# Token-layout block sums and DMA transposes between the output projection and the up projection

## The chip, the cores and the metric

The kernel runs on one core of a Trainium2 chip. TensorE multiplies, VectorE and ScalarE compute element by element, GpSimd does a few small steps and SyncE (SP) issues most DMAs. Each engine runs its own instructions in order and waits on semaphores for the others. The metric is the device time of one execution in microseconds (us), as the median of several timed runs.

## The reference

One layer of a decoder trunk on x of 1024 tokens by 1024 channels, in float32. What matters here is the seam between the two halves of the layer:

```
merged = sigmoid(g_att) * y_att + sigmoid(g_conv) * y_conv
x = x + rms_norm(merged @ w_out, norm_mix_post)        # output projection

h = rms_norm(x, norm_ffn_pre)
u = causal_dwconv(h @ w_up, conv_ffn_w)                # up projection, 1024 -> 5632
a, g = split(u)
x = x + rms_norm((gelu(g) * a) @ w_down, norm_ffn_post)
```

## The kernel before

**Numbers.** Operands of a product are kept as two float16 parts, a high and a low half: the high half is the value times a power of two (ScalarE writes it), the low half what is left (VectorE writes it). A product takes three passes (high·high, high·low, low·high), so 12 matmuls of 512 columns for a 512x512 block and 128 output channels.

**The up projection** uses seven block products in place of eight. The normalized h is wanted with channels on the partitions: hA holds, in four quadrants (channel half by token half), the plain blocks B11, B21, B22 and the sum T4; hB holds the sums T1, T2, T3. T1 is late minus early tokens of the first channel half, T2 is the second channel half of the late tokens minus T1, T4 the second channel half of the early tokens minus T2, T3 the difference of the late tokens' channel halves. Tokens come in eight tiles of 128: tiles 0 to 3 are the early half, 4 to 7 the late one; tile 4 pairs with tile 0, and so on. `Pair.prod(i)` is one block product; prod(1) and prod(2) read the early quadrants of hA, prod(5), (6) and (7) read T1, T2, T3, prod(3) and prod(4) the late quadrants of hA.

**The stage around the change.** For each tile, `out_proj` runs 48 matmuls into two PSUM banks (py), reading m16_0 to m16_7 (the merged activations) and wo_0 to wo_7 (the weights), in the order of k for each half of the columns. ScalarE squares (L861), VectorE evicts with the gain into hn (L862), r_post comes from GpSimd, x2 is the new residual (L866), stored by SP, and hn becomes the normalized h (L869). `load_xr` fetches the next tile's x on SP.

`blocks(tt, h)` turns that tile: eight TensorE transposes of 128x128 into two PSUM banks (pt), then for an early tile halves written straight into hA (L885, L886), for a late tile the sums T1 to T4 in channel layout, from PSUM and from hA (L893 to L903), with their halves. The list of tiles in the loop sets where the blocks stand: `{2: (0,), 3: (1,), 4: (2,), 5: (3, 4), 6: (5,), 7: (6,)}`, and tile 7's come after the first products of pairs u0 and u1. A scheduler orders the instructions of each engine by its own timeline; the program's order gives the dependences.

**Memory.** `slot()` takes a 4 KB-per-partition tile from one pool, the slab:

```
self.slab = top.enter_context(tc.tile_pool(name="slab", bufs=16))
...
wo_pools = (self.slab, "s", self.slab, "s")
```

At this stage the slab holds the eight tiles of wo, m16_4 to m16_7, the hn tiles, the work tiles of the blocks (tb, hb) and s12, a sum over the weights of the next pair (L969 to L971). A tile gets a slot when an earlier tenant has had its last reader. PSUM has eight banks (pool pz), shared by py, pt and the products (pu).

Of the kernel before, what the change touches and what calls it, by code (L numbers as in the profile page):

```python
# [16 lines left out]
F16 = mybir.dt.float16  # L17
BF16 = mybir.dt.bfloat16
F32 = mybir.dt.float32
I32 = mybir.dt.int32  # L20
AF = mybir.ActivationFunctionType
ALU = mybir.AluOpType
AX = mybir.AxisListType

P = 128
T = 1024
D = 1024
KD = D // P
NH = 512
# [4 lines left out]
KH = KD // 2  # L34
# [3 lines left out]
class Layer:  # L38
# [225 lines left out]
    def mixer(self, mid):  # L264
        tc, nc, a = self.tc, self.nc, self.a
        hT = self.hp.tile([P, 2, KD, T], F16, tag="hT", name="hT")
        with ExitStack() as ph1:
# [33 lines left out]
            with tc.tile_pool(name="ptp", bufs=2, space=bass.MemoryType.PSUM) as ptp:  # L301
                gb = self.slot([P, D], F32, "g_pre")
                xt, rt, pt = {}, {}, {}
# [426 lines left out]
        with ExitStack() as ph2:  # L730

            hB = self.h7p.tile([P, 2, 3, KH, NH], F16, tag="hB", name="hB")
            t4s = []

            def halves(dst, src):
                nc.scalar.activation(dst[:, 0], src, AF.Copy)
                nc.vector.tensor_tensor(dst[:, 1], src, dst[:, 0], ALU.subtract)

            def blocks(q):
                lo, hi = ds(0, NH), ds(NH, NH)  # L740
                kA, kB = ds(2 * q, 2), ds(KH + 2 * q, 2)

                def diff(name, p, m, hT_m=True):

                    t = self.slot([P, 2, NH], F32, f"{name}_{q}")
                    nc.vector.tensor_tensor(t, hT[:, 0, p[0], p[1]], hT[:, 0, m[0], m[1]] if hT_m else m,
                                            ALU.subtract)
                    nc.vector.tensor_tensor(t, t, hT[:, 1, p[0], p[1]], ALU.add)
                    if hT_m:
                        nc.vector.tensor_tensor(t, t, hT[:, 1, m[0], m[1]], ALU.subtract)  # L750
                    return t
                t1 = diff("T1", (kA, hi), (kA, lo))
                halves(hB[:, :, 0, ds(2 * q, 2), :], t1)
                t2 = diff("T2", (kB, hi), t1, False)
                halves(hB[:, :, 1, ds(2 * q, 2), :], t2)
                t4s.append(diff("T4", (kB, lo), t2, False))
                t3 = diff("T3", (kB, hi), (kA, hi))
                halves(hB[:, :, 2, ds(2 * q, 2), :], t3)
# [19 lines left out]

            branches(0, 1, bi=0)
            blocks(0)  # L780
            branches(2, 3, bi=0)
            self.pair_fetch("g1")
            self.inv_h = inv_h
            blocks(1)
            for which in ("gc", "ga"):
                nc.scalar.activation(sig[which, 0], sig[which, 0], AF.Sigmoid)
# [12 lines left out]
            for d in range(1, 8):  # L799
                p = gp[d]  # L800
# [48 lines left out]
        def out_proj(tt):  # L849
# [19 lines left out]
            nc.vector.scalar_tensor_tensor(h, y, r2, gf, ALU.mult, ALU.mult)  # L869
            return h  # L870

        def blocks(tt, h):


            pt = [self.bank(f"pt{tt}_{e}") for e in range(2)]
            for k in range(KD):
                nc.tensor.transpose(pt[k // KH][:, ds((k % KH) * P, P)], h[:, ds(k * P, P)], self.ident)
            sl = ds((tt % 4) * P, P)
            p3 = [p.rearrange("p (k t) -> p k t", k=KH) for p in pt]
            s2 = ds(NH + (tt % 4) * P, P)  # L880
            b11, b21, b22, t4 = hA[:, :, :KH, sl], hA[:, :, KH:, sl], hA[:, :, KH:, s2], hA[:, :, :KH, s2]
            t1, t2, t3 = [hB[:, :, e, :, sl] for e in range(3)]
            if tt < 4:
                for p, b in zip(p3, (b11, b21)):
                    nc.scalar.activation(b[:, 0], p, AF.Copy, scale=s_h2)  # L885
                    nc.vector.scalar_tensor_tensor(b[:, 1], p, s_h2, b[:, 0], ALU.mult, ALU.subtract)  # L886
                return
            tb = [self.slot([P, 2, KH, P], F32, f"tb{tt}_{e}") for e in range(2)]

            def halves(dst, src):  # L890
                nc.scalar.activation(dst[:, 0], src, AF.Copy)
                nc.vector.tensor_tensor(dst[:, 1], src, dst[:, 0], ALU.subtract)
            nc.vector.scalar_tensor_tensor(tb[0][:, 0], p3[0], s_h2, b11[:, 0], ALU.mult, ALU.subtract)  # L893
            nc.vector.tensor_tensor(tb[0][:, 0], tb[0][:, 0], b11[:, 1], ALU.subtract)
            halves(t1, tb[0][:, 0])
            nc.vector.scalar_tensor_tensor(tb[0][:, 1], p3[1], s_h2, tb[0][:, 0], ALU.mult, ALU.subtract)
            halves(t2, tb[0][:, 1])
            hb = self.slot([P, 2, KH, P], F32, f"hb{tt}")
            for e in range(2):
                nc.scalar.activation(hb[:, e], p3[e], AF.Copy, scale=s_h2)  # L900
            nc.vector.tensor_tensor(tb[1][:, 0], hb[:, 1], hb[:, 0], ALU.subtract)
            nc.vector.tensor_tensor(tb[1][:, 1], b21[:, 0], tb[0][:, 1], ALU.subtract)
            nc.vector.tensor_tensor(tb[1][:, 1], tb[1][:, 1], b21[:, 1], ALU.add)  # L903
            halves(b22, hb[:, 1])
            halves(t3, tb[1][:, 0])
            halves(t4, tb[1][:, 1])

        xr = {}

# [4 lines left out]
        hs = {}  # L914
        load_xr(0)
        for tt in range(8):
            if tt + 1 < 8:
                load_xr(tt + 1)
            hs[tt] = out_proj(tt)
            if tt == 0:  # L920
                self.pair_split("u0")
                self.pair_fetch("u1")
            if tt == 3:
                self.pair_sums("u1")
                self.pair_split("u1")
            if tt == 4:
                self.pair_fetch("u2")
            for t in {2: (0,), 3: (1,), 4: (2,), 5: (3, 4), 6: (5,), 7: (6,)}.get(tt, ()):
                blocks(t, hs[t])
# [356 lines left out]
```

## Time and profile before

| what | value |
|---|---|
| timed runs | 1368.22, 1368.27, 1367.43 us; median 1368.22 |
| profiled execution, its own time from first to last instruction (span) | 1365.7 us |
| TensorE busy | 1336.1 us, 98% |
| VectorE busy | 1028.6 us, 75% |
| ScalarE busy | 860.7 us, 63% |
| TensorE's mean granted clock | 0.998 |
| transposes between the projections (L877) | 64 of 272 ns each, started 664.2 to 735.0 |

The times in a profile run from the span's start. A row of a timeline names the start, how long it took, the engine, the line, the operation and what it writes from what. "Busy" of TensorE counts pipelined matmuls that overlap, so the step from one matmul to the next is shorter than its duration. Waits are put down to the engine whose signal came last.

### The profile page before, as it was taken

The page shows a single profiled execution, that of the slowest core. Times are in us where ns is not written, and L with a number is a line of the kernel's source. Part 1 is how long each engine was busy: PE and PEld are TensorE (multiplying, and loading weights), DVE is VectorE, ACT ScalarE, POOL GpSimd, SP SyncE. Part 2 cuts the span into 40 slices and gives each one's busy share as a digit, 9 for nine tenths or more (in the row PEclk, how much of TensorE's full clock was granted, in tenths as well). Part 3 has the DMA queues.
Part 4 walks back from the last instruction along what each step waited for, and adds up shares of the span by engine and source line. Part 5 has one row for each costly group of instructions (what it writes and reads, how often), then busy time and mean ns, then how long its engine had stood idle before and what let it go on. Part 6 is the DMA issues. An engine that isn't in the chain of part 4 may idle for free. (4 is left out here: it accounts for less than half of the span.)

```text
span 1365.7 us, 16990 instructions
## 1 busy us (share of the span) xinstructions
PE 1336.1 (98%) x6651; PEld 607.7 (44%) x6651; DVE 1028.6 (75%) x1610; ACT 860.7 (63%) x1204; POOL 34.2 (3%) x52
## 2 busy tenths in 40 slices
PE   6999999999999999999999999999999999999997
PEld 3444444444444444444454444444444444444443
DVE  6667777777775965878788985984894896699855
ACT  6668778787775775666466577652761673476524
POOL 2000000000000000000010000000000000000002
PEclk9999999999999999999999999999999999999999
DMA  7102111101111121351331123122220321313216
GB/s 264 62 1 62 32 31 32 38 25 39 40 31 47 32 62 31 93 185 36 119 124 62 62 62 123 39 87 85 70 78 16 123 62 62 109 45 124 63 46 109
DMA packets 26576, 96.06 MB, mean 70 GB/s; under 512 B 3072, under 2 KB 3200, under 8 KB 26496
## 3 DMA queue, kind: packets, MB, share of 16 engines
q1 hardware_dynamic: 25056, 89.74, 20.3%
q0 software_dynamic: 1440, 5.24, 2.1%
q8 instruction: 52, 0.85, 0.2%
q14 instruction: 28, 0.23, 0.1%
HBM read 86.58 MB, written 8.39 MB: 70 GB/s over the span
## 5 line engine op out<-in xcount | busy, mean ns | idle before, releaser
L1156 PEld LDWEIGHTS <-wh_u 128*128 128x128 f16 x1848 | 178.8, 98 | 217.3 <-issue 3.5
L1048 PE MATMUL pd<-wdh,f 128*128 128x512 f16 (+1 forms) x1068 | 230.3, 377 | 2.8 <-ACT wdh L86 1.2
L1048 PEld LDWEIGHTS <-f 128*128 128x128 f16 x1068 | 104.4, 98 | 127.2 <-issue 4.3
L86 ACT ACTIVATE wh_u<-ws_u,sc 128x1024 f16<-128x1024 f32 (+1 forms) x66 | 64.7, 998 | 102.9 <-DVE sc L78 79.3
L1055 DVE SCALAR_TENSOR_TENSOR yacc<-pd,sd,yacc 128x512 f32<-128x512 f32 (+1 forms) x81 | 58.5, 740 | 72.7 <-PE pd L1048 65.2
L1156 PEld LDWEIGHTS <-wh_g 128*128 128x128 f16 x588 | 56.9, 98 | 68.7 <-issue 0.4
L859 PE MATMUL py<-wh_wo,m 128*128 128x512 f16 x384 | 83.9, 379 | 0.0
L87 DVE SCALAR_TENSOR_TENSOR wh_u<-ws_u,sc,wh_u 128x1024 f16<-128x1024 f32 (+1 forms) x66 | 72.1, 1099 | 9.5 <-ACT wh_u L86 9.4
L643 DVE SCALAR_TENSOR_TENSOR w<-zc,w 128x1024 f16<-128x1024 f32 (+3 forms) x48 | 45.7, 955 | 34.5 <-ACT w L642 34.4
L622 ACT ACTIVATE sp<-zc 128x1024 f32<-128x1024 f32 (+3 forms) x48 | 40.2, 838 | 46.7 <-DVE zc L615 29.1
L600 PE MATMUL A<-sh,tri 128*128 128x512 f16 (+3 forms) x352 | 67.8, 322 | 0.0
L1233 DVE SCALAR_TENSOR_TENSOR ugu<-cgu,cw_g,ugu 128x1023 f32<-128x1023 f32 (+1 forms) x44 | 56.2, 1278 | 11.3 <-ACT ugu L1231 10.9
L1233 DVE SCALAR_TENSOR_TENSOR ua<-cau,cw_a,ua 128x1023 f32<-128x1023 f32 (+1 forms) x44 | 56.1, 1276 | 1.4 <-ACT ua L1231 1.3
L859 PEld LDWEIGHTS <-m 128*128 128x128 f16 x384 | 37.5, 98 | 44.1
L626 DVE TENSOR_TENSOR sh<-sp,sh 128x1024 f16<-128x1024 f32 (+3 forms) x48 | 45.7, 952 | 12.9 <-ACT sh L625 12.7
L640 ACT ACTIVATE zc<-zc 128x1024 f32<-128x1024 f32 (+3 forms) x48 | 40.0, 834 | 15.4 <-DVE zc L638 15.0
L638 DVE SCALAR_TENSOR_TENSOR zc<-A,zc 128x1024 f32<-128x1024 f32 (+3 forms) x48 | 45.5, 949 | 2.3 <-PE A L600 2.3
L56 ACT ACTIVATE jk_u<-ws_u 128x1024 bf16<-128x1024 f32 x44 | 46.4, 1054 | 0.9
L200 PE MATMUL pk<-hT,wh_k 128*128 128x512 f16 x192 | 46.8, 380 | 0.0
L200 PE MATMUL pq<-hT,wh_q 128*128 128x512 f16 x192 | 44.3, 379 | 1.3 <-DVE sc L79 1.3
L623 ACT ACTIVATE sp<-sp,one 128x1024 f32<-128x1024 f32 (+3 forms) x48 | 44.6, 928 | 0.8
L200 PE MATMUL pcb<-hT,wh_cb 128*128 128x512 f16 x192 | 44.8, 379 | 0.0
(620 smaller groups left out, 2606.4 us busy)
## 6 DMA issues: line engine op xcount, KB each, us to landing
ws_u<-w_up_nt SPq DMA_DIRECT2D x44, 512.0 KB, 3.7
ds<-w_down SPq DMA_DIRECT2D x22, 512.0 KB, 6.1
wd<-w_down SPq DMA_DIRECT2D x22, 512.0 KB, 3.7
ws_g<-w_in_nt SPq DMA_DIRECT2D x14, 512.0 KB, 3.6
x<-x SPq DMA_DIRECT2D x8, 512.0 KB, 8.0
ws_wo<-w_out SPq DMA_DIRECT2D x8, 512.0 KB, 7.1
xr<-x SPq DMA_DIRECT2D x8, 512.0 KB, 4.3
out<-x SPq DMA_DIRECT2D x7, 512.0 KB, 2.9
```

The lines of the kernel that those rows point to most:

```text
L56: self.nc.scalar.activation(self.junk(f"jk_{name}"), src, AF.Square, accum_out=acc)
L86: self.nc.scalar.activation(dst[:, 0, :], src, AF.Copy, scale=s)
L87: self.nc.vector.scalar_tensor_tensor(dst[:, 1, :], src, s, dst[:, 0, :], ALU.mult, ALU.subtract)
L200: nc.tensor.matmul(ps, w[:, wi, ds(k * P, P)], hT[:, hi, k, ds(c * NH, NH)], start=n == 0, stop=n == last)
L600: nc.tensor.matmul(out, w, mv, skip_group_check=True, **kw)
L626: nc.vector.tensor_tensor(sh[:, 1, :, off:], sp[:, :, off:], sh[:, 0, :, off:], ALU.subtract)
L643: nc.vector.scalar_tensor_tensor(w[:, 1, :, off:], zc[:, :, off:], 2.0 ** 14, w[:, 0, :, off:], ALU.mult, ALU.subtract)
L859: nc.tensor.matmul(ps, m16[k][:, hi, ds(tt * P, P)], wo[k][:, wi, sl], start=k == 0 and p == 0, stop=k == 7 and p == 2)
L1048: nc.tensor.matmul(pd[nh], f16[g][k][:, hi, ds(tt * P, P)], w[k][:, wi, ds(*part)], start=run is runs[0] and n == 0, stop=run is runs[-1] ...
L1055: nc.vector.scalar_tensor_tensor(y[:, sl], ps, sm[:, 0:1], y[:, sl], ALU.mult, ALU.add)
L1156: nc.tensor.matmul(ps, w[wt][:, wi, ds(wc * NH + k * P, P)], self.block(i, hi, k), start=first and n == 0, stop=n == 3 * KH - 1, skip_grou ...
L1233: nc.vector.scalar_tensor_tensor(u[:, lag:], c[:, :T - lag], sm[:, 2 - lag:3 - lag], u[:, lag:], ALU.mult, ALU.add)
```

## The change

Sums and halves are taken with tokens on the partitions, from hn itself, and the float16 halves are turned by DMA transposes issued from SP into the same places of hA and hB. An early tile has two of them (high, low), of 1024 columns. A late tile takes T1 and T2 into one work tile, T4 and T3 into another, makes halves of T1|T2, T4|B22 and T3, and issues six transposes. The late tile reads the early tile's hn (`hs[tt - 4]`) where it read hA before. The halves are written into nt tiles in the slab. The TensorE transposes of this stage and their PSUM tiles are gone; those at the start of the kernel stay.

```diff
+        def turn(dst, src):
+            nc.sync.dma_start_transpose(dst, src)
+
         def blocks(tt, h):
-            pt = [self.bank(f"pt{tt}_{e}") for e in range(2)]
-            for k in range(KD):
-                nc.tensor.transpose(pt[k // KH][:, ds((k % KH) * P, P)], h[:, ds(k * P, P)], self.ident)
...
+            def halves(dst, src):
+                nc.scalar.activation(dst[:, 0], src, AF.Copy, scale=s_h2)
+                nc.vector.scalar_tensor_tensor(dst[:, 1], src, s_h2, dst[:, 0], ALU.mult, ALU.subtract)
+
             if tt < 4:
-                for p, b in zip(p3, (b11, b21)):
-                    nc.scalar.activation(b[:, 0], p, AF.Copy, scale=s_h2)
-                    nc.vector.scalar_tensor_tensor(b[:, 1], p, s_h2, b[:, 0], ALU.mult, ALU.subtract)
+                n = self.slot([P, 2, D], F16, f"nt{tt}")
+                halves(n, h)
+                for hl in range(2):
+                    turn(hA[:, hl, :, sl], n[:, hl])
                 return
...
+            h0 = hs[tt - 4]
+            lo, hi = ds(0, NH), ds(NH, NH)
+            tb = [self.slot([P, D], F32, f"tb{tt}_{e}") for e in range(2)]
+            n = [self.slot([P, 2, D], F16, f"nt{tt}_{e}") for e in range(3)]
+            nc.vector.tensor_tensor(tb[0][:, lo], h[:, lo], h0[:, lo], ALU.subtract)
+            nc.vector.tensor_tensor(tb[0][:, hi], h[:, hi], tb[0][:, lo], ALU.subtract)
+            halves(n[0], tb[0])
+            for hl in range(2):
+                turn(hB[:, hl, :2, :, sl].rearrange("p e k t -> p (e k) t"), n[0][:, hl])
+            nc.vector.tensor_tensor(tb[1][:, lo], h0[:, hi], tb[0][:, hi], ALU.subtract)
+            halves(n[1][:, :, lo], tb[1][:, lo])
+            halves(n[1][:, :, hi], h[:, hi])
+            for hl in range(2):
+                turn(hA[:, hl, :, s2], n[1][:, hl])
+            nc.vector.tensor_tensor(tb[1][:, hi], h[:, hi], h[:, lo], ALU.subtract)
+            halves(n[2][:, :, lo], tb[1][:, hi])
+            for hl in range(2):
+                turn(hB[:, hl, 2, :, sl], n[2][:, hl, lo])
```

More of the change, by code (lines that the diff above doesn't have):

```diff
@@ L870, in out_proj @@
             return h
+        def turn(dst, src):
+            nc.sync.dma_start_transpose(dst, src)
         def blocks(tt, h):
-            pt = [self.bank(f"pt{tt}_{e}") for e in range(2)]
-            for k in range(KD):
[L877 to L881, printed above, removed]
@@ L882, in blocks @@
-            t1, t2, t3 = [hB[:, :, e, :, sl] for e in range(3)]
+            sl, s2 = ds((tt % 4) * P, P), ds(NH + (tt % 4) * P, P)
+            def halves(dst, src):
+                nc.scalar.activation(dst[:, 0], src, AF.Copy, scale=s_h2)
+                nc.vector.scalar_tensor_tensor(dst[:, 1], src, s_h2, dst[:, 0], ALU.mult, ALU.subtract)
             if tt < 4:
-                for p, b in zip(p3, (b11, b21)):
-                    nc.scalar.activation(b[:, 0], p, AF.Copy, scale=s_h2)
-                    nc.vector.scalar_tensor_tensor(b[:, 1], p, s_h2, b[:, 0], ALU.mult, ALU.subtract)
+                n = self.slot([P, 2, D], F16, f"nt{tt}")
+                halves(n, h)
+                for hl in range(2):
+                    turn(hA[:, hl, :, sl], n[:, hl])
@@ L887, in blocks @@
                 return
[L888 to L903, printed above, removed]
@@ L904, in blocks @@
-            halves(b22, hb[:, 1])
-            halves(t3, tb[1][:, 0])
-            halves(t4, tb[1][:, 1])
+            h0 = hs[tt - 4]
[4 more added lines that the diff above has]
+            nc.vector.tensor_tensor(tb[0][:, hi], h[:, hi], tb[0][:, lo], ALU.subtract)
```

## The prediction

> **What bounds the kernel now.** I read the page's busy table first, then the windows around the output projection, TensorE's timeline there, its waits, and last the groups by shape.
>
> ```profile
> span 1365.7 us, 16990 instructions
> PE 1336.1 (98%) x6651; PEld 607.7 (44%) x6651; DVE 1028.6 (75%) x1610; ACT 860.7 (63%) x1204; POOL 34.2 (3%) x52
> ```
>
> TensorE is busy 98% of the span, so a microsecond that it loses shows in the time. The three timed runs have a median of 1368.22; the profiled execution spans 1365.7, and I take the 2.5 us around it as unchanged. 0.2% is 2.7 us, about what a measurement of this kernel tells from no change.
>
> ```profile
> 700.00:710.00 10.00, 10.00 (x48) 4.44 (x47) 9.56 (x17) 6.73 (x13) 2.62 (x2) 1.00 0.32 105
> 710.00:720.00 10.00, 10.00 (x52) 5.04 (x52) 9.96 (x18) 6.69 (x13) 1.46 (x2) 1.00 0.28 90
> 720.00:730.00 10.00, 8.64 (x44) 4.20 (x43) 9.96 (x19) 6.13 (x12) 1.11 (x2) 1.00 0.24 79
> 730.00:740.00 10.00, 8.01 (x41) 3.95 (x40) 9.13 (x17) 7.72 (x15) 1.05 (x1) 1.00 0.12 44
> 740.00:750.00 10.00, 10.00 (x49) 4.55 (x48) 4.72 (x12) 3.25 (x6) 0.00 (x0) 1.00 0.01 2
> ```
>
> The columns are time, then busy time of TensorE, its weight loads, VectorE, ScalarE and GpSimd, TensorE's granted clock, DMA share and GB/s. VectorE is full from 700 to 730 (9.56, 9.96, 9.96 of 10): it works through the tiles' epilogues and blocks while TensorE multiplies. Between 720 and 740 TensorE idles 3.35 us. The changed stage is thus one where VectorE has no room, but still runs beside TensorE.
>
> ```profile
> 664.18 1.04 PE L877 MATMUL pt<-ident,hn 128*128 128x128 f32 x8
> 665.05 10.52 PE L859 MATMUL py<-wh_wo,m 128*128 128x512 f16 x48
> ...
> 675.44 1.07 PE L877 MATMUL pt<-ident,hn 128*128 128x128 f32 x8
> ...
> 686.71 1.04 PE L877 MATMUL pt<-ident,hn 128*128 128x128 f32 x8
> ...
> 697.94 1.91 PE L877 MATMUL pt<-ident,hn 128*128 128x128 f32 x16
> ...
> 710.05 1.04 PE L877 MATMUL pt<-ident,hn 128*128 128x128 f32 x8
> 710.92 10.52 PE L859 MATMUL py<-wh_wo,m 128*128 128x512 f16 x48
> 722.06 1.09 PE L877 MATMUL pt<-ident,hn 128*128 128x128 f32 x8 [0.61 <-DVE hn L869]
> 722.99 2.75 PE L1156 MATMUL pu0a<-hA,wh_u 128*128 128x512 f16 x12
> ...
> 731.66 2.75 PE L1156 MATMUL pu1a<-hA,wh_u 128*128 128x512 f16 x12
> 734.25 1.04 PE L877 MATMUL pt<-ident,hn 128*128 128x128 f32 x8
> 737.08 0.38 PE L1156 MATMUL pu0c<-hB,wh_u 128*128 128x512 f16 x1 [1.79 <-ACT hB L891]
> ...
> 737.87 2.53 PE L1156 MATMUL pu0c<-hB,wh_u 128*128 128x512 f16 x11 [0.20 <-DVE hB L892]
> ```
>
> Tile 7's 48 projection matmuls start at 710.92 and end at 721.44. Four products of the first two pairs need only hA and cover the last blocks; the first that needs the last tile's T1 (pu0c) runs freely from 737.87. That row is the mark I compare with: after it nearly nothing waits.
>
> ```profile
> PE pd L1048 <- ACT wdh L86: 1.2, 2, 0.7
> PE pd L1048 <- DVE cau L1183: 1.0, 1, 1.0
> PE pd L1048 <- DVE wdh L87: 0.6, 1, 0.6
> ```
>
> These are all of TensorE's named waits from 780 to the end, 2.8 us. A delay at pu0c is carried to the end, but for at most these 2.8.
>
> **TensorE, removed.** A group of eight transposes holds it from 664.18 to 665.05, 0.87 us; eight groups are 7.0 us. Six lie ahead of tile 7's projection (the row of 16 is two), 5.2 us; so in the changed kernel that projection starts at 705.7, its second half 24 matmuls later at 710.9 (a matmul steps by (10.52 − 0.38)/47 = 0.216 us), and it ends at 716.2. Two of eight PSUM banks come free as well.
>
> **Slots, added.** This is the step that decides. Blocks of tiles 4 to 7 now subtract hs[tt-4], so hn0 to hn3 must live until the block four tiles later; before, a tile's hn died with its transposes. They come from the slab, which has 16 slots: eight hold wo and four m16_4 to m16_7, all until the projection's end. hn0, hn1, hn2 and nt0 take the other four; hn3 takes nt0's slot once its two transposes have landed. Then none is free until wo_0 is read for the last time, by the third matmul of tile 7's second half. In the built order of the changed kernel the next takers on VectorE and ScalarE are s12_u1, nt1, hn4 and nt2, and the built addresses give them the slots of wo_0, wo_1, wo_2 and wo_3. VectorE runs in order: right behind tile 4's r_post it stands before s12_u1, and behind it are queued the evictions of tiles 4 to 7 (L862), all x2 stores and residuals from tile 4 on, and every block from tile 1 on. ScalarE stands before nt1 with its copies behind it. TensorE goes on, for tiles 4 to 7 need eight banks and there are eight. So nearly everything that ran beside the projections runs after them: VectorE starts at 710.9 + 3 × 0.216 + a matmul's own 0.38 us, less one step, or about 711.8.
>
> **VectorE, the work then in line.** The rows are groups by shape, with the mean in ns behind the busy time.
>
> ```profile
> L862 DVE SCALAR_TENSOR_TENSOR hn<-py,sgn,g_post 128x512 f32<-128x512 f32 x16 | 11.7, 748 | 4.9 <-ACT jk_n_post L861 4.9
> L866 DVE SCALAR_TENSOR_TENSOR x<-hn,r_post,xr 128x1024 f32<-128x1024 f32 x8 | 10.3, 1282 | 2.1 <-POOL r_post L171 2.1
> L87 DVE SCALAR_TENSOR_TENSOR wh_u<-ws_u,sc,wh_u 128x1024 f16<-128x1024 f32 x4 | 5.0, 1278 | 0.0
> L894 DVE TENSOR_TENSOR tb<-tb,hA 128x512 f32<-128x512 f32 x4 | 2.7, 685 | 0.0
> L863 DVE TENSOR_TENSOR r_post<-r_post 128x1 f32<-128x1 f32 x8 | 1.2, 148 | 0.0
> L1230 DVE TENSOR_SCALAR cw_a<-cfw,sc,g_ffn 128x3 f32<-128x3 f32 x2 | 0.6, 279 | 0.0
> ```
>
> From s12_u1 to the low half of nt7_0 the built order has 17 three-operand passes of 1024 columns (seven low halves, four L866, four L869, two L87), 18 of 512 (eight L862, nine halves, one L87), 20 two-operand passes of 512 (four of u1's sums, four per block of tiles 4 to 7), three L1230 and 14 one-column ones: 17 × 1.28 + 18 × 0.747 + 20 × 0.685 + 3 × 0.28 + 14 × 0.15 = 51.8 us. Back to back an instruction starts some 0.08 us before its forerunner's end, which takes off 72 × 0.08 = 5.8; the round trips to GpSimd and ScalarE between r_post, x2, r_ffn and hn add about as much where nothing fills them (4.9 and 2.1 us in these rows). I keep 51.8, with 46 and 58 as ends: the low half of nt7_0 is ready at 763.6 (757.8 to 769.8).
>
> The change saves VectorE work: a late block was 2 × 0.747 + 9 × 0.685 = 7.7 us and is 4 × 0.685 + 3 × 0.747 + 1.28 = 6.3. That is inside the sum. ScalarE is the lighter engine (6.69 beside 9.96 in the window from 710) and follows.
>
> **DMA transposes, added.** 32 on SP's queue, which carried only copies; the trace of before has none.
>
> ```profile
> 667.65 0.34 SPq L867 DMA_DIRECT2D out<-x  x1
> ...
> out<-o SPq DMA_DIRECT2D x2, 256.0 KB, 2.6
> ...
> x<-x SPq DMA_DIRECT2D x8, 512.0 KB, 8.0
> cfw<-conv_ffn SPq DMA_DIRECT2D x1, 66.0 KB, 8.1
> ```
>
> Nearest by size is the 256 KB copy, 2.6 us to landing with some 0.4 of SP; farthest is cfw in short pieces, 8.1. From nt1's first to nt7_0's low half SP has 27 transposes and ten copies (x2 stores, xr6, xr7, u2 and u3 loads), in the 50 us from 713.7 on. Copies take 4; so as long as a transpose takes SP or the crossbar under (50 − 4)/27 = 1.7 us, VectorE sets the pace, and only the last one's 0.4 + 2.6 us is added: pu0c runs at 766.6. A gain from them below nothing is excluded, since TensorE's saving is counted above. I take the 256 KB row, overlapped as copies are.
>
> The Trainium skill ("DMA: Bandwidth & Descriptors", section Latency and other measured facts) gives a transposing DMA 261 GB/s with a non-contiguous middle dimension, an estimate of 1.0 us for 256 KB; by it the sum is the same. No run here shows it yet.
>
> **Sum.** 766.6 − 737.9 = 28.7 us later, less up to 2.8 of later waits, of which I take a quarter: 28. 1368.2 + 28 = **1396.2**. By VectorE's ends: 22.9 − 2.8 = 20 to 35.
>
> **Rivals.**
> *The transpose queue becomes the bound.* If a transpose lets the next go only when it has landed, 27 × 2.6 + 4 = 74 us from 713.7, pu0c at 788: +50, 1418. For it: the slots of nt4 and later are reused at once, so landings also hold VectorE. Against: SP's copies overlap.
> *Each transpose is as slow as short pieces.* 27 × 8.1 = 219 us, pu0c near 937: +199, about 1567. The skill's "VectorE: DVE Perf Modes" (The three transpose paths) speaks against this change: 1309 ns for a 128x128 block by DMA, 390 by TensorE; eight blocks in a row would be an estimated 10.5 us per transpose, in this regime.
> *Only part is held.* If tiles 4 and 5 were evicted beside the projection, two of four epilogues and blocks leave the line, 2 × (2 × 0.748 + 2 × 1.28 + 3 × 0.15 + 6.3) = 22 us: +6, 1374.
>
> *Faster.* Slots come free as before, and VectorE is never held at s12_u1.
>
> ```profile
> 731.46 1.27 DVE L869 SCALAR_TENSOR_TENSOR hn<-x,r_ffn,g_ffn 128x1024 f32<-128x1024 f32 x1
> ```
>
> Then hn7, ready at 732.7, 11.3 us after the projection, is ready at 727.5; two subtractions (1.4), ScalarE's and VectorE's halves (about 1.1 + 1.3) and a transpose (3.0) give pu0c at 734.3, 3.6 us earlier: 1364.6. It decides if the hold is under 3.6 us. Against it stands the count of slots.
>
> **Chances.** VectorE in line after the projections 0.66; transpose queue 0.20; short pieces 0.04; part held 0.05; faster 0.04, and 0.01 within 0.2%. So faster 0.04, same 0.01, slower 0.95. The range takes VectorE's ends and the queue up to +50: 1388 to 1419; outside are the short pieces, the part hold and faster.
>
> **What would show it.** Right: VectorE idle some 23 us, from about 688 (tile 4's projection ends near 685, its r_post some 3 us later) to 711.8, released by TensorE at L969; L862 of tile 4 after 711; TensorE's projections without a gap to 716; then TensorE idle some 35 us in stretches, ahead of pu0a (nt1 to nt3), behind its first product (whose eviction stands on ScalarE behind tile 6's halves) and ahead of pu0c; VectorE full from 712 to 763. Wrong: evictions of tiles 4 to 7 beside the projections; or VectorE and ScalarE waiting on transposes after 712, which is the queue; or transposes landing in over 4 us each.

## The result

| what | before | after |
|---|---|---|
| time, median of the runs | 1368.24 us (4 runs, 1367.43 to 1369.01) | 1403.87 us (4 runs, 1402.93 to 1404.99) |
| span of the profiled execution | 1365.7 us | 1401.2 us |
| TensorE's mean granted clock | 0.998 | 0.983 |

After over before is 1.026, with a 95% interval of 1.0246 to 1.0275. Of the 35.6 us the profiled spans show 35.5.

The page of the changed kernel, its span and busy table:

```profile
span 1401.2 us, 16923 instructions
PE 1337.4 (95%) x6587; PEld 602.4 (43%) x6587; DVE 1024.5 (73%) x1594; ACT 855.6 (61%) x1188; POOL 32.5 (2%) x52
```

No computing engine got more to do: VectorE has 4 us less than before, ScalarE 5 less, and TensorE's 64 transposes are gone (its busy time is 1.3 us more all the same, as some matmuls ran at a lower clock). The span grew by idle time. The windows of the changed kernel, with the columns of the windows before:

```profile
690.00:700.00 10.00, 10.00 (x48) 4.57 (x47) 0.00 (x0) 0.00 (x0) 0.00 (x0) 1.00 0.01 2
710.00:720.00 10.00, 5.81 (x27) 2.45 (x25) 8.65 (x11) 6.06 (x7) 0.00 (x0) 1.00 0.51 98
720.00:730.00 10.00, 0.00 (x0) 0.00 (x0) 5.43 (x10) 4.86 (x10) 0.55 (x1) 0.54 0.65 216
750.00:760.00 10.00, 2.91 (x7) 1.01 (x7) 9.56 (x17) 6.14 (x10) 1.40 (x2) 0.50 1.01 204
780.00:790.00 10.00, 10.00 (x48) 4.51 (x47) 4.71 (x7) 3.14 (x4) 0.00 (x0) 1.00 0.00 0
```

From 690 to 700 TensorE is full, and VectorE, ScalarE and GpSimd stand at 0.00. Later it is the other way round: TensorE has 0.00 from 720 to 730 and 2.91 from 750 to 760, where VectorE has 9.56. Work that ran side by side runs one after the other. The clock column falls to 0.50 where TensorE idles. VectorE's timeline in the changed kernel shows the stand (its long wait at L969), its two later waits of over 3 us, and the low half of nt7_0, tile 7's first staging tile:

```profile
686.92 0.15 DVE L170 TENSOR_SCALAR r_post<-r_post 128x1 f32<-128x1 f32 x1
711.31 0.69 DVE L969 TENSOR_TENSOR s_u<-ws_u 128x512 f32<-128x512 f32 x1 [24.23 <-PE py L859]
...
727.25 0.15 DVE L68 TENSOR_REDUCE sc<-sm_u 128x1 f32<-128x2 f32 x1 [3.35 <-ACT jk_u L56]
...
764.46 0.16 DVE L68 TENSOR_REDUCE sc<-sm_u 128x1 f32<-128x2 f32 x1 [4.16 <-ACT jk_u L56]
...
767.39 1.28 DVE L881 SCALAR_TENSOR_TENSOR nt<-tb,g_ffn,nt 128x1024 f16<-128x1024 f32 x1
```

And TensorE's timeline there, from the last tiles' projections on:

```profile
674.21 41.60 PE L859 MATMUL py<-wh_wo,m 128*128 128x512 f16 x192
732.93 0.61 PE L1156 MATMUL pu0a<-hA,wh_u 128*128 128x512 f16 x1 [17.12 <-DMA hA<-nt]
...
757.09 5.00 PE L1156 MATMUL pu0a<-hA,wh_u 128*128 128x512 f16 x12 [13.98 <-ACT cgu L1171]
...
770.71 0.59 PE L1156 MATMUL pu0c<-hB,wh_u 128*128 128x512 f16 x1 [6.04 <-DVE nt L881]
...
773.42 4.88 PE L1156 MATMUL pu0c<-hB,wh_u 128*128 128x512 f16 x11 [0.82 <-DMA hB<-nt]
```

The mark, pu0c running freely, was at 737.87 and is at 773.42: 35.55 us later, as much as the whole span grew.

The staging tiles in the changed kernel (SP's rows give count and duration in ns, least, median and most; the last line is from a transpose's issue to its landing):

```profile
L873 SPq DMA_TRANSPOSE hA<-nt x16: 1231/1266/1613, 671.0 to 771.4; - x16
L873 SPq DMA_TRANSPOSE hB<-nt x16: 1217/1233/3302, 733.3 to 774.1; - x16
...
DMA to landing us min/median/max: 2.4/3.2/6.1
```

### The profile page after: what moved, and what is told of

The parts are those of the page before. It is cut to its first block, busy times and chain, and to the rows that moved or that the text cites. A ratio compares the mean times of both kernels' runs of the same rounds, so it can differ in the third digit from the quotient of the medians.

```text
span 1401.2 us, 16923 instructions
## 1 busy us (share of the span) xinstructions
PE 1337.4 (95%) x6587; PEld 602.4 (43%) x6587; DVE 1024.5 (73%) x1594; ACT 855.6 (61%) x1188; POOL 32.5 (2%) x52
## 2 busy tenths in 40 slices
DMA packets 56272, 103.40 MB, mean 74 GB/s; under 512 B 32768, under 2 KB 32896, under 8 KB 56192
## 4 chain that ended last, share of the span: by engine, by line
PE 85%; DVE 5%; ACT 3%; DMA 2%; issue 1%; POOL 0%; SPq 0%; POOLq 0%; DVEq 0%; ACTq 0%
PE pd L1048 16%; PE py L859 6%; PE A L600 4%; PE pcb L200 3%; PE pcx L200 3%; PE pywa L580 3%; PE pcc L200 3%; PE pywc L580 3%; PE o L600 2%; PE pk L200 2%; PE pq L200 2%; PE z L600 2%; PE pv L343 1%; DMA ws_u<-w_up_nt 1%; PE pgc L200 1%
## 5 line engine op out<-in xcount | busy, mean ns | idle before, releaser
L1156 PEld LDWEIGHTS <-wh_u 128*128 128x128 f16 x1848 | 180.6, 99 | 261.6 <-issue 31.6
L859 PE MATMUL py<-wh_wo,m 128*128 128x512 f16 x384 | 83.1, 379 | 0.0
L859 PEld LDWEIGHTS <-m 128*128 128x128 f16 x384 | 37.4, 98 | 45.1
L1231 ACT ACTIVATE ua<-cau,cw_a 128x1024 f32<-128x1024 f32 x22 | 25.1, 1140 | 32.3 <-DVE cau L1183 27.1
```

What stands on the lines that cost most here:

```text
L859: nc.tensor.matmul(ps, m16[k][:, hi, ds(tt * P, P)], wo[k][:, wi, sl], start=k == 0 and p == 0, stop=k == 7 and p == 2)
L1156: nc.tensor.matmul(ps, w[wt][:, wi, ds(wc * NH + k * P, P)], self.block(i, hi, k), start=first and n == 0, stop=n == 3 * KH - 1, skip_grou ...
```

## The experiments

Two theories at first. *Slots:* hn0 to hn3 and the staging tiles take the slab's slots, so VectorE and ScalarE stand until wo is read for the last time. *Transposes:* the 32 transposes on SP's queue cost the time. Later, for what the slots left over, two more, *load* and *clock*: a wait for a weight load among the transposes, and TensorE's clock after an idle stretch. The medians of before beside these runs were 1367.6, 1368.8 and 1368.2 us; each difference is taken to its own.

**The early tiles' hn freed early.**

```diff
-            h0 = hs[tt - 4]
+            h0 = h
```

> The changed kernel, with one line of blocks other: a late tile's sums are taken from its own hn alone (h0 = h), so the values of the early tile are left out of T1, T2 and T4. Every instruction, transpose and size stays; but hn0 to hn3 are dead after their own blocks, so their slots come free as before the change. Slot theory (VectorE and ScalarE stand because hn0 to hn3 and the staging tiles hold the slots that s12_u1 and nt1 need, until wo is read for the last time): the stand of 24 us at L969 goes; the next one is hn6 (L862), which in the built order gets the slot of wo_1 and so still waits for tile 7's second half, near 711. Then two tiles' epilogues and blocks are in line behind it instead of four: the changed kernel less two of them, 2 x (2 x 0.748 + 2 x 1.28 + 3 x 0.15 + 6.3) = 22 us: 1382, pu0c freely from about 752; between 1374 and 1390. Transpose theory (the 32 transposes on SP's queue cost the time): 1398 to 1404, pu0c at 768 or later, as all 32 are still there.

Measured 1380.17 us, 12.6 over before (ratio 1.0092, 1.0077 to 1.0107); pu0c runs freely from 751.75. 23 of the 35 us go with the slots of four tiles, and all transposes are still there. The stand at L969 is gone, as VectorE's timeline of this run shows:

```profile
698.10 1.28 DVE L881 SCALAR_TENSOR_TENSOR nt<-hn,g_ffn,nt 128x1024 f16<-128x1024 f32 x1 [3.34 <-ACT nt L880]
...
714.73 0.69 DVE L898 TENSOR_TENSOR tb<-hn,tb 128x512 f32<-128x512 f32 x1 [3.10 <-DMA hB<-nt]
...
742.74 0.15 DVE L68 TENSOR_REDUCE sc<-sm_u 128x1 f32<-128x2 f32 x1 [3.90 <-ACT jk_u L56]
```

But hn6's expected wait for wo isn't among VectorE's waits. Among what is left are other waits: one for u3's load (3.90 us), and waits for landings, since a staging tile's slot comes free only when its transpose has landed. ScalarE's timeline in the same run:

```profile
696.92 1.15 ACT L880 ACTIVATE nt<-hn,g_ffn 128x1024 f16<-128x1024 f32 x1 [7.23 <-DMA hA<-nt]
```

The size was right, the wait behind it wasn't the one named.

**Plain copies in place of the transposes.**

```diff
-            nc.sync.dma_start_transpose(dst, src)
+            nc.sync.dma_start(dst, src.rearrange("p (k t) -> p k t", t=P))
```

> The changed kernel with each of the 32 DMA transposes replaced by a plain DMA copy of the same block to the same place, its columns taken in the order of the destination, so that what is left out is the turning alone (the products then read blocks that are not transposed). Slots, sums and order stay. Slot theory: the stand at L969 stays at about 24 us and the time falls only by what the transposes themselves cost, the last one's 4.8 us to pu0c against some 3 and the two waits on u2's and u3's sums: 1394 to 1404. Transpose theory: most of the 35 us goes, 1368 to 1380.

Measured 1401.12 us, 33.5 over before (1.0246, 1.0229 to 1.0263). That is some 2 us less than the change itself, with intervals that overlap, so the turning itself costs little. VectorE's stand in this run, and the staging tiles' rows:

```profile
711.05 0.69 DVE L969 TENSOR_TENSOR s_u<-ws_u 128x512 f32<-128x512 f32 x1 [24.21 <-PE py L859]
```

```profile
L873 SPq DMA_DIRECT2D hA<-nt x16: 593/600/1231, 670.8 to 767.9; - x16
L873 SPq DMA_DIRECT2D hB<-nt x16: 594/667/2452, 732.3 to 769.0; - x16
...
DMA to landing us min/median/max: 2.3/3.5/7.2
```

A copy of the same block holds SP half as long as a transpose (600 beside 1266 ns), and lands no sooner (3.5 beside 3.2 us). Halving SP's hold moved the time little, so the time that SP takes for each transpose isn't what sets the end: VectorE still stands 24.21 us at L969. The transposes theory falls.

**Before, with hn0 and hn1 kept alive.**

```diff
             if tt < 4:
...
                 return
+            if tt in (4, 5):
+                keep = self.small(f"keep{tt}")
+                nc.vector.tensor_copy(keep[:, 0:1], hs[tt - 4][:, 0:1])
```

> The kernel before the change, with one added VectorE instruction of one column in the blocks of tiles 4 and 5, which reads hn0 and hn1, so that these two stay alive until then as they must in the changed kernel. Nothing else is changed: TensorE transposes, sums and values are those of before. Slot theory: two of four free slots are gone; in the built order hb5 (ScalarE) and a tb5 (VectorE) get the slots of wo_0 and wo_1 and wait for tile 7's second half, now near 717, some 5 us later than they ran; 1370 to 1376, with a wait on L859 of 3 to 8 us on VectorE that before had not. Transpose theory, and the theory that the order of the sums matters: 1367.5 to 1369, since nothing of these is in it.

Measured 1374.87 us, 7.3 over before (1.0053, 1.0038 to 1.0068): keeping two tiles costs time without any DMA transpose. But the expected wait on L859 isn't there. In VectorE's timeline before, u1's first sum stands ahead of tile 3's second eviction:

```profile
678.46 0.68 DVE L969 TENSOR_TENSOR s_u<-ws_u 128x512 f32<-128x512 f32 x1
```

In this run it stands at

```profile
687.20 0.69 DVE L972 TENSOR_TENSOR s_u<-ws_u 128x512 f32<-128x512 f32 x1
```

with pair u1's splits behind it, and TensorE's timeline of this run shows who waits for that:

```profile
700.81 1.06 PE L877 MATMUL pt<-ident,hn 128*128 128x128 f32 x8 [2.44 <-DVE hn L869]
...
733.55 4.44 PE L1159 MATMUL pu0a<-hA,wh_u 128*128 128x512 f16 x12 [3.74 <-ACT cgu L1174]
```

With fewer slots the scheduler had put u1's sums behind tile 3's work, into the full stretch: the price came through the order, not through a semaphore. That the missing slots made it choose so is argued, not shown.

**The early tiles alone by DMA.**

```diff
             if tt < 4:
                 n = self.slot([P, 2, D], F16, f"nt{tt}")
...
-            h0 = hs[tt - 4]
...
+            pt = [self.bank(f"pt{tt}_{e}") for e in range(2)]
+            for k in range(KD):
+                nc.tensor.transpose(pt[k // KH][:, ds((k % KH) * P, P)], h[:, ds(k * P, P)], self.ident)
...
```

> Half of the change alone: tiles 0 to 3 are staged in token layout (nt) and turned by 8 DMA transposes; tiles 4 to 7 are turned by TensorE and summed in block layout as before the change, so no early hn is kept. Slot theory: hn0 to hn3 die at their blocks and s12_u1 waits only for a transpose's landing (some 3 us), so the stand of 24 us is not there; 1366 to 1372, pu0c freely between 736 and 741. Transpose theory: a quarter of the 32 transposes, so about a quarter of 35 us: 1374 to 1380.

Measured 1371.85 us, 4.3 over before (1.0031, 1.0019 to 1.0043), inside the slot theory's times; pu0c at 743.72 is later than it allowed. ScalarE stands 7.29 us before one staging tile until an earlier one's transpose has landed:

```profile
698.76 1.15 ACT L879 ACTIVATE nt<-hn,g_ffn 128x1024 f16<-128x1024 f32 x1 [7.29 <-DMA hA<-nt]
```

VectorE stands behind it, and so hn4 is late for TensorE:

```profile
703.29 1.97 PE L886 MATMUL pt<-ident,hn 128*128 128x128 f32 x8 [6.20 <-DVE hn L869]
705.05 12.21 PE L859 MATMUL py<-wh_wo,m 128*128 128x512 f16 x48
```

After that idle stretch the 48 matmuls take 12.21 us, where 10.52 is their time elsewhere.

**The early hn kept elsewhere.** hn0 to hn3 are parked as fp32 in the half of hA that the late tiles fill; the second version makes the sums in place there.

```diff
-            h = self.slot([P, D], F32, f"hn{tt}")
+            if tt < 4:
+                h = hA.bitcast(F32)[:, :, :, ds(NH // 2 + tt * (P // 2), P // 2)]
+            else:
+                h = self.slot([P, D], F32, f"hn{tt}").rearrange("p (a k t) -> p a k t", a=2, k=KD)
...
-            tb = [self.slot([P, D], F32, f"tb{tt}_{e}") for e in range(2)]
+            tb = full(self.slot([P, D], F32, f"tb{tt}"))
```

> The whole change, computing all that the reference needs, but hn0 to hn3 are kept as fp32 in the half of hA that tiles 4 to 7 fill later (each in the columns that its own late tile overwrites) instead of in four slab slots; the late tiles use one tb slot instead of two, and T4's difference is made in hn's own slot. Slot theory: s12_u1 and nt1 get slots without waiting for wo, so the stand of 24 us goes, as with the early hn freed; what is left in the built order are nt4_1 (ScalarE, the slot of wo_0) and hn6 (VectorE, the slot of wo_2), which wait until 711 or so: 1377 to 1385, pu0c freely at 749 to 756. Transpose theory: 32 transposes as before, so 1396 or more.

> As the parked version, but the late tiles' sums are made in place over the parked hn0 to hn3 (in pieces of 64 columns) and only T2's difference has a slab slot, of half the size. One more slot is free per late tile: hn6 no longer waits for wo, but nt4_1 on ScalarE still does. Slot theory: 1 to 4 us less than the parked version, 1375 to 1382; if the remaining loss is in the transposes' landings and u3's load and not in slots, the same as the parked version within 1 us.

Measured 1382.43 us, 13.6 over before (1.0102, 1.0087 to 1.0117), and 1380.31 us, 11.5 over (1.0086, 1.0071 to 1.0101). So the change keeps a loss of about 12 us with the hold gone, as in the run that freed them; no version here beats the kernel before. The waits for wo that were still expected aren't in either timeline. In the parked version the last block still waits for landings, as VectorE's timeline says:

```profile
747.81 0.69 DVE L906 TENSOR_TENSOR tb<-hn,hA 128x512 f32<-128x512 f32 x1 [3.38 <-DMA hA<-nt]
```

Whether this wait comes through the slot of its work tile or through hA, where hn3 is parked, isn't shown. The parking adds waits of its own: the write of hn3 into hA stood 2.74 us for a transpose into hA. So these 12 us aren't all of one cause.

**u3's loads put off**, in two steps: behind hn7, then behind the last staging tile.

```diff
             blocks(7, hs[7])
+        self.praw["u3"] = self.wfetch("u3", self.psrc["u3"], after=hs[7])       # first run
+        self.praw["u3"] = self.wfetch("u3", self.psrc["u3"], after=last[7][:, 1])  # second: nt7's last tile
...
-                if 1 <= f and f + 2 < NFF:
+                if 2 <= f and f + 2 < NFF:
```

> The changed kernel with only the two loads of pair u3 put off until hn7 is there (a one-column VectorE copy from hn7 ahead of each load). Load theory: some 4 us of the changed kernel's loss are VectorE's wait for ScalarE's sum of a u3 load (L68 behind jk_u, 4.16 us ahead of tile 7's block), a load that stood behind transposes on SP's queue and landed 5 us later; with it gone the low half of nt7_0 is ready some 4 us earlier, near 764.7, and pu0c runs freely near 769 to 770: 1399 to 1401. If this wait only fills time that another limit (SP's transposes) sets anyway, pu0c stays at 773 and the time at 1403 to 1405.

Measured 1401.15 us, 32.3 over before (1.0243, 1.0226 to 1.026). VectorE had the low half of nt7_0 at 764.3 (763.06 + 1.28), as the load theory said, but pu0c's first matmul was no sooner:

```profile
770.74 0.59 PE L1157 MATMUL pu0c<-hB,wh_u 128*128 128x512 f16 x1 [6.79 <-DMA hB<-nt]
...
772.42 3.33 PE L1157 MATMUL pu0c<-hB,wh_u 128*128 128x512 f16 x11
```

SP's timeline of this run has the likely reason, the two loads right ahead of tile 7's first transposes:

```profile
763.64 1.01 SPq L103 DMA_DIRECT2D ws_u<-w_up_nt  x2
764.74 4.77 SPq L873 DMA_TRANSPOSE hB<-nt  x2
```

The profiled span is 2.6 us less than the changed kernel's all the same. The 11 further matmuls of pu0c started 1.0 us earlier (0.5 of it because the stand ended earlier in this execution), and they took 3.33 us in place of 4.88: most of this gain is TensorE's clock, not the load.

The second run puts the loads behind all transposes, with the unaltered change beside it.

> The changed kernel once more, unaltered, beside the two that follow, so that differences of 2 or 3 us are taken on one chip. Every theory: 1402 to 1405.

> The changed kernel with u3's two loads put off until the last staging tile of tile 7 is written, so that on SP's queue they stand behind all 32 transposes. In the run that put them off until hn7, VectorE had the low half of nt7_0 ready at 764.3 instead of 768.7, but u3's loads then stood ahead of tile 7's first transpose and pu0c still waited 6.8 us for hB. Load theory: with both gone pu0c's second matmul runs at 767 to 769 instead of 773.4, and the time is 1397 to 1400, unless u3's later sum brings a new wait on VectorE. If SP's transposes of tiles 5 and 6 alone hold tile 7's, pu0c stays at 771 or later: 1401 to 1403.

Measured 1403.35 us (35.1 over before) and 1399.78 us, 31.6 over (1.0234, 1.022 to 1.0247): 3.6 us less. VectorE's and TensorE's timelines of the second:

```profile
710.13 0.69 DVE L971 TENSOR_TENSOR s_u<-ws_u 128x512 f32<-128x512 f32 x1 [24.24 <-PE py L859]
...
762.47 1.28 DVE L881 SCALAR_TENSOR_TENSOR nt<-tb,g_ffn,nt 128x1024 f16<-128x1024 f32 x1 [1.03 <-ACT nt L880]
```

```profile
766.33 0.38 PE L1158 MATMUL pu0c<-hB,wh_u 128*128 128x512 f16 x1 [2.97 <-DVE nt L881]
...
767.08 0.59 PE L1158 MATMUL pu1b<-hB,wh_u 128*128 128x512 f16 x1
769.00 4.88 PE L1158 MATMUL pu0c<-hB,wh_u 128*128 128x512 f16 x11 [1.34 <-DMA hB<-nt]
```

pu0c is 4.4 us earlier than in the changed kernel, 1.2 of it because VectorE's stand ended earlier in this run (710.13 beside 711.31). The load theory holds for this wait, worth some 3 us.

**TensorE kept busy.**

```diff
         p1.prod(2)
+        ps = self.bank("warm")
+        for k in range(30):   # 22 in the second run
+            nc.tensor.matmul(ps[:, ds(0, 3 * P)], self.pw["u0"][0][0][:, 0, ds(0, P)], hB[:, 0, 0, 0, ds(0, 3 * P)], start=True, stop=True)
         p0.prod(5)
```

> The changed kernel with 30 more matmuls of 384 columns, which read the parts of hB that tiles 4 to 6 have filled and write a bank that nobody reads; on TensorE they stand ahead of the second products of the first two pairs (22) and ahead of pu0c (8), in time that TensorE idles in. Clock theory: the half granted clock after an idle stretch costs pu0c's 11 matmuls 4.88 instead of 2.53 us, 2.4 us in all; with TensorE busy up to pu0c they take 2.53 and the time falls to 1401 to 1402. If the clock does not depend on what TensorE did just before, or the added work delays pu0c itself, the time is 1403 to 1408 and the 11 still take over 4 us.

> As the run before it, with 22 of the added matmuls of 384 columns ahead of the second products of the first two pairs, so that TensorE hardly idles before pu0c. Clock theory: another 2 to 2.4 us less, since pu0c's 11 matmuls take 2.5 us instead of 4 to 5: 1395 to 1398. Otherwise the same as the run before it, or later by what the added matmuls hold pu0c back.

Measured 1404.05 us (1401.15 to 1405.21), 35.2 over before, and 1403.02 us, 34.8 over. In the first run pu0c's 11 matmuls are fast again:

```profile
768.17 1.46 PE L940 MATMUL warm<-hB,wh_u 128*128 128x384 f16 x8
770.75 0.39 PE L1159 MATMUL pu0c<-hB,wh_u 128*128 128x512 f16 x1 [1.12 <-DVE nt L881]
...
773.48 2.55 PE L1159 MATMUL pu0c<-hB,wh_u 128*128 128x512 f16 x11 [1.67 <-DMA hB<-nt]
```

The clock theory is right about the matmuls: 2.55 us in place of 4.88 at the same place. In the profiled execution the gain reaches the end: the product behind pu0c (pu1c) starts 2.2 us earlier than in the changed kernel, and the span is 1398.9, 2.3 less (0.5 of it from an earlier end of the stand). But the other executions of this run span 1400.1 to 1403.5 and the median shows no gain; why is open. The second run missed: the added matmuls held back the first pair's second product (763.70 beside 756.02), its eviction stands on ScalarE ahead of tile 7's halves, and VectorE waited 4.45 us for nt7_0's high half; pu0c came at 774.25, again after idle stretches and again in 4.88 us.

## Why the prediction was right, and where its sizes were off

The prediction was 1396.2 us with 1388 to 1419; measured were 1403.87. The slot theory's own ends were 20 to 35 us, and 35.6 were lost: the measured time lies just above its end, in the part of the range that was there for the transpose queue. So the mechanism was right, and that the range held owes something to room taken for a theory that fell.

**Slots, the deciding step: right.** VectorE was to stand some 23 us, from 688 to 711.8, at L969, released by TensorE. It stood 24.23 us and started at 711.31. Projections without a gap to 716, the idle stretches ahead of pu0a, behind its first product and ahead of pu0c, and evictions of the late tiles after 711 are in the trace. Freed or parked, the early hn take 22 to 24 us of the loss with them.

**VectorE's line: work right, waits missing.** From 711.31 to the end of the low half of nt7_0 (767.39 + 1.28 = 768.67) it took 57.4 us, against 51.8 (46 to 58 as bounds). The two waits for ScalarE's sums of u2's and u3's loads, 3.35 and 4.16 us, are 7.5 of it; without them 49.9. The prediction let the round trips fill what overlap saved. It counted u2's and u3's loads as copies on SP, and L68 among VectorE's short instructions, but put no wait between them: x2's store, the transposes and these loads share SP, and L68 stands behind them. Put off, u3's wait is gone and the line takes 53.6 us (710.13 to 763.75).

**The last transpose: mis-sized.** Taken from the 256 KB copy at 3.0 us, it is 773.42 − 768.67 = 4.75. SP had just begun another of tile 7's transposes (768.68, 1.29 us), issued this one at 770.06, and TensorE ran 3.36 us later, where 2.6 had been taken. The bound of 1.7 us for SP per transpose did hold (1.23 and 1.27 in the median), and SP's hold isn't the bound, as the plain copies show.

The Trainium skill ("DMA: Bandwidth & Descriptors", section Latency and other measured facts) gave 261 GB/s, an estimate of 1.0 us for 256 KB; the hold of 1.27 us is 207 GB/s, and a transpose of half the size held SP as long, so here it isn't a matter of bytes alone. The Trainium skill's "VectorE: DVE Perf Modes" (The three transpose paths) has 1309 ns for one 128x128 block by DMA; as a price for each block it doesn't carry over either: eight blocks in one DMA hold SP for 1.27 us and land in 3.2.

**The sum.** 1.75 from the transpose and 5.6 from the line, less the 0.5 of an earlier start, make the 6.8 us by which pu0c (773.42) missed 766.6. Behind it, TensorE's clock is a term the prediction didn't have: 4.88 in place of 2.53 for pu0c's 11 matmuls, 2.35 us. Against it stand later waits, as TensorE's waits in the changed kernel from 780 on show:

```profile
PE pd L1048 <- ACT wdh L86: 0.7, 2, 0.5
PE pd L1048 <- DVE wdh L87: 0.6, 1, 0.6
```

They are 1.3 us in place of 2.8, 1.5 given back where 0.7 was taken. Three small terms more: pu1c's 11 matmuls still begin slow, 2.86 us in place of 2.54; two more matmuls than before had run ahead of the mark, 0.4 us; and what follows TensorE's last matmul is 0.5 us shorter. 35.55 + 2.35 + 0.3 − 1.5 − 0.4 − 0.5 = 35.8 beside 35.5 measured.

**The rivals.** The queue as the bound and the short pieces are out by the plain copies and by the holds; the partial hold (1374) by the stand; the faster case (1364.6) by the count of slots. That case doesn't come even without the hold: the three versions without it stay 11 to 14 us over before. In the one that freed the early hn, staging tiles wait for landings, and the wait for u3's load and the low clock are still there; how the 12 us split between them is open.

## What to carry to other kernels

Before a sum is moved to another layout, list how long each operand must now live and which pool it lives in: four tiles kept for four tiles longer cost more here than the transposes, the engine work and the queue together. A DMA transpose frees its staging tile only when it lands, so a chain through few slots pays a landing for each link, 3.2 us in the median here, where a group of TensorE transposes took 0.87 us. And when one queue takes over a stage, look for the transfers of the next stage that stand in it.

## What the runs showed of the hardware

A DMA transpose between tiles in SBUF held SP for some 1.25 us whatever its size: hA's 16, all of 1024 columns, have a median of 1.27, hB's 16, half of them of 512 columns, 1.23. It landed after 3.2 us in the median; a plain copy of the same block, in rows of 128 float16 values, held SP for 0.6 us and landed after 3.5. In the changed kernel 32768 packets are under 512 B, 3072 before:

```profile
DMA packets 56272, 103.40 MB, mean 74 GB/s; under 512 B 32768, under 2 KB 32896, under 8 KB 56192
```

A 512 KB weight load issued among the transposes was there for ScalarE 5.6 us later (issued 757.68, its sum at 763.27), against a median of 3.5 us for such loads in the whole kernel:

```profile
ws_u<-w_up_nt SPq DMA_DIRECT2D x44, 512.0 KB, 3.5
```

After idle stretches TensorE starts at half its rate: (4.88 − 0.59)/10 = 0.43 us a matmul beside 0.216. The Trainium skill ("TensorE: Matmul & The Clock Gate", section Part 1: The HAM clock gate (the "warmup" mystery)) says that the clock is halved after an idle window of about 3.4 us and released after as long a busy one. The half agrees; the full rate was back some 5 us after pu0c's 11 matmuls began at 773.42, within pu1c's. As to the window, in the run with u3's loads last TensorE idled 2.97 us, ran pu0c's first matmul at full rate (0.38 us) and was at half by the fourth (0.59), 3.7 us after the idle began, so the clock fell though matmuls had resumed. The parked version kept the full clock after an idle stretch of 2.31 us:

```profile
754.47 0.38 PE L1169 MATMUL pu0c<-hB,wh_u 128*128 128x512 f16 x1 [2.31 <-DMA hB<-nt]
...
755.59 2.54 PE L1169 MATMUL pu0c<-hB,wh_u 128*128 128x512 f16 x11
```
